# Where the last two projection steps stand among the token mixers' steps of a hybrid encoder

## Chip, cores and metric

The kernel runs on one core of a Trainium2 chip. The metric is the device time of one execution in microseconds (us), as a median over runs. Engines are called as in the profile: PE (TensorE matmuls), PEld (TensorE weight loads), DVE (VectorE), ACT (ScalarE), POOL (GpSimd), SP (SyncE, which issues most of the DMAs here).

## What is computed

Two layers, each over 512 tokens of width 1024. A layer projects its input x with one matrix `w_in`, gives the parts to three token mixers, joins their outputs with a second matrix, and ends in a mixture of experts. Cut to what matters here:

```python
for l in range(DEPTH):                                   # DEPTH = 2
    p = x @ w_in[l]
    c_q, c_kv, k_r, m_q, m_k, m_v, m_o, m_g, s_z, s_xbc, s_dt = split(p)
    y_a = mla(c_q, c_kv, k_r, ...)                       # attention, 8 heads
    y_b = mlstm(m_q, m_k, m_v, m_o, m_g, ...)            # ends: y = sigmoid(m_o) * layernorm(h)
    y_c = ssd(s_z, s_xbc, s_dt, ...)                     # ends: y = rmsnorm(y * silu(z)) over 2 groups
    x = layernorm(alpha * x + concat(y_a, y_b, y_c) @ w_out[l])
    x = layernorm(alpha * x + experts(x))
```

## The kernel before

Tokens are cut into NT = 4 tiles of 128. The transposed input x lies in the SBUF tensor `xt` (16 parts: 8 blocks of 128 features, each as a high part `xh[k]` and a rest `xl[k]`), and each fp32 product is built of three fp32r matmuls (high times high, high times rest, rest times high). All other large data live in 37 SBUF slots `s0` to `s36` (the profile calls them all `s`), handed out first in, first out; a slot taken from the pool and given back later in the program text is waited for by its next user. PSUM has 8 banks (`b` in the profile): banks 0 to 2 (`PA`) for projections and attention's inputs, banks 3 to 7 (`PB`) for the SSD, which the mLSTM (`PM`, banks 3 and 4) and attention's scores (`PT_`, banks 5 to 7) use after it.

The mixers are generator functions. One string, `SEQ`, written out by hand, says which generator goes one step further; it is the same for both layers:

```python
streams = {"d": ssd(), "p": projections(), "m": mlstm(), "i": mla_in(), "h": ssd_heads()}
for n, t in enumerate(SEQ):
    if t == "s" and "s" not in streams:
        streams["s"], streams["v"] = attention()
    next(streams[t], 1)
for t in "dphmisv":
    assert next(streams[t], 1) == 1
```

What the steps are (d17 is the 17th d of the string):

- d1 to d19, `ssd()`: d1 to d8 and d10 to d17 each take one token tile in one direction (ACT exponentials, a DVE product with the matrix C·B, two PE products into the bank `py`); d9 and d18 close a group (DVE: `y = x*d + py`, then `y * z2`; ACT: its square); d19 is the norm: `rms_cols` (one-column matmuls against `ones`), the DVE chain `rsqrt_`, `row_bc` (matmuls against `ident` that spread the result over partitions) and two DVE products. A d20 has nothing left to do.
- p1 to p11, `projections()`: p8 and p9 make mLSTM's v, two token tiles each, and p10 and p11 make `tho`, the tanh of mLSTM's output gate, two token tiles each: `proj_tm` is 24 matmuls of 256 columns per tile out of `xt` (written `b<-s,xt` in the profile), then an ACT tanh. At its begin p10 gives back the weights of v, fetches and splits the gate's weights. Its load from DRAM is issued at p8. A p12 only gives the four slots of the gate's weights back.
- i1 to i3, `mla_in()`: i1 holds the two `rms_cols` of attention's inputs, i2 loads and splits `w_ukv`, i3 makes the values `vt` (four times three matmuls of 512 columns, four ACT copies) and the router's sums. An i4 has nothing left to do.
- h1, `ssd_heads()`: splits the two SSD outputs into `xt` blocks 6 and 7, which p11 must have read to its end.
- m: mLSTM's 22 steps; m1 transposes the keys, the last one normalises and multiplies with `tho`. s and v: attention's scores and values, 40 steps each.

After the mixers the output projection `w_out` follows, then the router and the experts.

The order in which a single engine meets the instructions is laid out ahead of time by the framework's planner, for which the text's order is a rank among instructions that are ready by its own estimates; so the queue of an engine need not have the text's order.

Of the kernel before, what the change touches and what calls it, by code (L numbers as in the profile page):

```python
# [68 lines left out]
MA = 3  # L69
NM = 2  # L70
SSD_STEPS = 19
SEQ = 'dpddpdpdpddpdddpdpddpiddpidpiddpddphimmssmsmssmsvmsvvsmsvsmsmvssvsvvsvmmvsvsvsmvmsvsmsvmsvsvmvvsvmmsvsvsmssvvmsmsvsvmsvsvsvvssvsvvsvsvvvvvv'

ROPE_INV = [1.0, 0.5623413324356079, 0.3162277638912201, 0.17782793939113617, 0.10000000149011612,
            0.05623413249850273, 0.03162277489900589, 0.017782794311642647, 0.009999999776482582,
# [137 lines left out]
def tile_trunk(ctx: ExitStack, tc: tile.TileContext, ins, out, dbg=None, depth=DEPTH):  # L213
# [46 lines left out]
    def ph(n):  # L260
        if PHASE:
            PHASE(n)
            if n != lastp[0]:
                lows[lastp[0]] = [min(a, b.low) for a, b in zip(lows.get(lastp[0], [99] * 4), (pool, PA, PB))]
                pool.low, PA.low, PB.low = len(pool.whole), 9, 9
            if n == "comb":
                print(lows)
            lastp[0] = n
# [290 lines left out]
    for l in range(depth):  # L559
# [424 lines left out]
        def ssd_heads():  # L984
            for g in range(2):
                finish_heads(6 + g, yz[g].ap)
                yz[g].free()
            yield
# [404 lines left out]
        streams = {"d": ssd(), "p": projections(), "m": mlstm(), "i": mla_in(), "h": ssd_heads()}  # L1393
        for n, t in enumerate(SEQ):
            ph({"m": "mlstm", "d": "ssd", "p": "proj"}.get(t, "attn"))
# [834 lines left out]
```

## Time and profile before

| | |
|---|---|
| median of 3 runs | 1066.05 us (1061.36 to 1069.1) |
| profiled execution | 1070.26 us, span 1067.8 us, mean granted clock 0.974 |
| PE, PEld busy | 93%, 69% of the span |
| DVE, ACT, POOL busy | 78%, 60%, 25% of the span |
| DMA | mean 166 GB/s over the span |

A busy PE is not a PE at its peak, since matmuls overlap. The mixers' part that this document is about runs from some 110 to 288 us in the first layer, and from some 635 to 814 us in the second.

### The profile page before, as it was taken

To read this page: it belongs to the slowest core of one execution; us is meant where nothing else is said; L and a number is where in the kernel's file an instruction comes from. 1 tells how busy PE (TensorE), PEld (TensorE's weight loads), DVE (VectorE), ACT (ScalarE), POOL (GpSimd) and SP (SyncE) were. 2 spreads that over 40 slices of the span, in tenths; PEclk is the share of its full clock that TensorE was granted. 3 is DMA by queue.
4 is the path that set the end of the run, shared out by engine and by line. 5 is a ranking of instruction groups with operands and counts; after the bars stand their busy time and mean duration, and the time that the engine had idled before them with its cause. 6 is when DMAs were issued, how large, how long until landed. Compare 5 with 4: busy or idle time off the path is not lost. (4 is left out here: it accounts for less than half of the span.)

```text
span 1067.8 us, 15553 instructions
## 1 busy us (share of the span) xinstructions
PE 996.5 (93%) x5310; PEld 739.2 (69%) x5310; DVE 836.0 (78%) x1832; ACT 644.6 (60%) x1182; POOL 267.2 (25%) x232
## 2 busy tenths in 40 slices
PE   6999999988998999999999999999799989999995
PEld 6876788555687666666598768876466876666653
DVE  8995557787749799999969955577876498999996
ACT  5565646555524588888646564466464347778874
POOL 1000002223003255565100000022220123556652
PEclk9999989998999899999999998999999989999998
DMA  7211100132656889996532120011347477999933
GB/s 305 69 45 45 40 21 21 35 126 99 234 198 218 282 288 345 335 324 213 204 139 70 40 69 1 21 40 41 118 138 246 168 275 264 311 339 337 308 94 155
DMA packets 51795, 176.76 MB, mean 166 GB/s; under 512 B 8169, under 2 KB 8681, under 8 KB 51712
## 3 DMA queue, kind: packets, MB, share of 16 engines
q1 hardware_dynamic: 45216, 160.42, 42.2%
q0 software_dynamic: 6496, 15.31, 6.0%
q8 instruction: 42, 0.69, 0.3%
q14 instruction: 41, 0.34, 0.1%
HBM read 159.61 MB, written 23.59 MB: 172 GB/s over the span
## 5 line engine op out<-in xcount | busy, mean ns | idle before, releaser
L230 PE MATMUL b<-xt,s 128*128 128x512 f32 (+3 forms) x1484 | 327.1, 367 | 13.8 <-ACT s L230 8.6
L230 PE MATMUL b<-s,s 128*128 128x512 f32 (+7 forms) x1308 | 324.7, 404 | 14.0 <-ACT s L230 7.1
L230 PEld LDWEIGHTS b<-xt,s 128*128 128x128 f32 (+2 forms) x1484 | 234.0, 183 | 80.3 <-issue 11.5
L230 DVE TENSOR_TENSOR s<-s,s 128x1024 fp32r<-128x1024 f32 (+8 forms) x254 | 247.6, 1000 | 50.5 <-ACT s L230 41.7
L230 PEld LDWEIGHTS b<-s,s 128*128 128x128 f32 (+3 forms) x1308 | 185.0, 173 | 99.7 <-DVE s L230 22.6
L230 ACT ACTIVATE s<-b 128x512 f32<-128x512 f32 (+8 forms) x282 | 135.0, 496 | 191.2 <-PE b L230 182.3
L230 ACT ACTIVATE s<-s 128x1024 fp32r<-128x1024 f32 (+5 forms) x219 | 191.6, 910 | 85.1 <-DVE s L230 31.8
L230 PE MATMUL b<-s,xt 128*128 128x256 f32 (+2 forms) x944 | 209.1, 362 | 0.4 <-POOL s L1523 0.4
L230 PEld LDWEIGHTS b<-s,xt 128*128 128x128 f32 (+1 forms) x944 | 150.6, 192 | 34.7 <-issue 4.8
L230 DVE TENSOR_TENSOR xt<-s,xt 128x1024 fp32r<-128x1024 f32 (+1 forms) x106 | 118.3, 1122 | 13.8 <-ACT xt L230 13.7
L230 ACT ACTIVATE xt<-s 128x1024 fp32r<-128x1024 f32 (+1 forms) x107 | 110.4, 1042 | 26.1 <-PE b L230 17.7
L230 PE MATMUL b<-ident,s 128*128 128x128 f32 (+3 forms) x736 | 107.4, 273 | 18.6 <-POOL s L1338 7.7
L230 PEld LDWEIGHTS b<-ident,s 128*128 128x128 f32 (+3 forms) x736 | 81.5, 153 | 53.3 <-ACT s L230 13.9
L1598 POOL DMA_INDIRECT acc<-s,slx x28 | 55.3, 1976 | 99.3 <-ACT s L230 79.4
L230 ACT ACTIVATE s<-b,mx,qsc 128x512 f32<-128x512 f32 x64 | 49.7, 782 | 25.5 <-DVE mx L230 25.1
L1338 POOL TENSOR_SCALAR s<-s,sums 128x512 f32<-128x512 f32 x48 | 37.6, 788 | 105.7 <-DVE sums L230 93.6
L1094 POOL MEMSET s<- 128x780 f32 x4 | 3.0, 756 | 219.9 <-DVE s L230 186.3
L230 DVE TENSOR_REDUCE mx<-b 128x1 f32<-128x512 f32 x64 | 43.2, 686 | 18.3 <-PE b L230 17.9
L1446 POOL DMA_INDIRECT s<-x1d,slx x30 | 40.5, 1351 | 57.4 <-PE b L230 23.0
L230 DVE TENSOR_TENSOR s<-b,s 128x192 fp32r<-128x192 f32 (+3 forms) x92 | 46.9, 524 | 4.6 <-POOL s L1127 2.6
L230 PE MATMUL b<-xt 128*96 128x512 f32 x160 | 48.0, 406 | 1.4 <-DVE xt L230 1.4
L230 ACT ACTIVATE s<-b,slw 96x512 f32<-96x512 f32 (+1 forms) x60 | 39.1, 682 | 14.9 <-PE b L230 8.3
(254 smaller groups left out, 983.9 us busy)
## 6 DMA issues: line engine op xcount, KB each, us to landing
s<-in_w_gu_dram SPq DMA_DIRECT2D x128, 512.0 KB
s<-in_expert_w_down_dram SPq DMA_DIRECT2D x64, 512.0 KB
s<-in_w_inp_dram SPq DMA_DIRECT2D x36, 512.0 KB
s<-in_w_outp_dram SPq DMA_DIRECT2D x16, 512.0 KB
x1d<-s SPq DMA_DIRECT2D x8, 512.0 KB
acc<-s SPq DMA_DIRECT2D x8, 512.0 KB
s<-acc SPq DMA_DIRECT2D x8, 512.0 KB
s<-in_x_t_dram SPq DMA_DIRECT2D x4, 512.0 KB
```

The source lines that it names most:

```text
L230: r = f(*a, **kw)
L1094: G.memset(cb.ap, 0.0)
L1338: (V if hd in NORMV else G).tensor_scalar(P.ap, P.ap, sums, 0.0, op0=OP.mult, op1=OP.add)
L1446: self.ga = G.indirect_dma_start(out=self.xg[:BLK], out_offset=None, in_=x1d[0:128 * n, :], in_offset=bass.IndirectOffsetOnAxis(ap=ix[:BLK ...
L1598: G.indirect_dma_start(out=acc[:, :], out_offset=bass.IndirectOffsetOnAxis(ap=self.ix[:BLK, 0:1], axis=0), in_=yt[:BLK], in_offset=None, b ...
```

## The change

Only the string changes. Steps that stand in both texts before and behind the changed stretch are left out here:

```diff
-SEQ = 'dpddpdpdpddpdddpdpddpiddpidpiddpddphimmssmsm...'
+SEQ = 'dpddpdpdpddpdddpdpddpiddpiddddpiphmmssmsm...'
```

With the steps numbered, the stretch behind i2 is

```
before: ... p9 i2 d16 p10 i3 d17 d18 p11 d19 d20 p12 h1 i4 m1 m2 s1 s2 ...
after:  ... p9 i2 d16 d17 d18 d19 p10 i3 p11 h1 m1 m2 s1 s2 ...
```

p10, i3 and p11 keep their order among themselves. d17 and d18 go ahead of p10 and i3, and d19 goes ahead of all three. d20, p12 and i4 leave the string; the loop behind it runs them when all steps of attention and mLSTM are written. So the four slots of the gate's weights, given back ahead of h1 before, are given back at the end of the mixers.

## Rows read from the trace of the kernel before

**Rows 1.** The page's first part: busy time, share of the span, instructions.

```profile
PE 996.5 (93%) x5310; PEld 739.2 (69%) x5310; DVE 836.0 (78%) x1832; ACT 644.6 (60%) x1182; POOL 267.2 (25%) x232
```

**Rows 2.** Busy time by stretch: us, engines, granted clock, DMA share, GB/s.

```profile
132.00:144.00 12.00, 12.00 (x77) 11.77 (x76) 5.11 (x31) 3.02 (x9) 0.00 (x0) 0.72 0.00 1
144.00:163.00 19.00, 19.00 (x140) 16.37 (x139) 9.31 (x20) 9.60 (x26) 0.76 (x1) 1.00 0.08 29
...
163.00:186.00 23.00, 22.31 (x141) 18.09 (x139) 18.23 (x50) 15.82 (x43) 5.96 (x9) 1.00 0.07 24
186.00:232.00 46.00, 44.10 (x240) 29.55 (x241) 36.45 (x103) 25.12 (x64) 12.24 (x17) 1.00 0.25 81
232.00:251.00 19.00, 12.93 (x40) 6.99 (x37) 15.87 (x36) 9.50 (x16) 6.01 (x4) 0.73 0.22 78
...
688.00:711.00 23.00, 21.46 (x132) 17.44 (x130) 16.33 (x47) 14.27 (x39) 5.88 (x9) 1.00 0.07 24
...
760.00:777.00 17.00, 10.89 (x37) 5.66 (x34) 14.01 (x34) 8.90 (x16) 5.39 (x4) 0.80 0.18 62
```

**Rows 3.** Timeline of PE, first layer: start, length, line, operation, count.

```profile
132.44 3.08 PE L230 MATMUL b<-ones,s 128*128 128x1 f32 x24
135.38 1.84 PE L230 MATMUL b<-s,xt 128*128 128x256 f32 x7
137.02 0.63 PE L230 MATMUL b<-s,sel 128*128 128x512 f32 x1
137.45 4.34 PE L230 MATMUL b<-s,xt 128*128 128x256 f32 x20
...
148.68 4.73 PE L230 MATMUL b<-s,xt 128*128 128x256 f32 x38
153.25 2.92 PE L230 MATMUL b<-s,s 128*128 128x512 f32 x12
...
156.25 1.08 PE L230 MATMUL b<-s,s 128*64 128x512 f32 x4
157.26 6.00 PE L230 MATMUL b<-s,xt 128*128 128x256 f32 x48
163.09 1.84 PE L230 MATMUL b<-ones,s 128*128 128x1 f32 x16
...
165.18 2.57 PE L230 MATMUL b<-s,s 128*128 128x512 f32 x11
167.67 2.05 PE L230 MATMUL b<-ident,rq_y 128*128 128x128 f32 x16
```

**Rows 4.** Timelines of DVE and ACT there; idle time ahead in brackets.

```profile
157.38 0.75 DVE L230 SCALAR_TENSOR_TENSOR s<-s,par,b 128x512 f32<-128x512 f32 x1 [0.76 <-PE b L230]
158.16 0.69 DVE L230 TENSOR_TENSOR s<-s,s 128x512 f32<-128x512 f32 x1
...
158.94 0.63 ACT L230 ACTIVATE s<-s 128x512 f32<-128x512 f32 x1 [2.14 <-DVE s L230]
...
164.97 0.17 DVE L230 TENSOR_SCALAR rms<-b 128x8 f32<-128x8 f32 x1 [2.19 <-PE b L230]
...
167.46 0.15 DVE L230 SCALAR_TENSOR_TENSOR rq_y<-rq_t,rq_y 128x8 f32<-128x8 f32 x1
...
169.02 1.48 DVE L230 SCALAR_TENSOR_TENSOR s<-s,par,b 128x512 f32<-128x512 f32 x2
...
171.07 0.68 DVE L230 TENSOR_TENSOR s<-b,rot 128x512 f32<-128x512 f32 x1
```

**Rows 5.** Timeline of PE: waits early and late in attention, first layer.

```profile
176.89 1.86 PE L230 MATMUL b<-s,s 128*128 128x128 f32 x11 [0.61 <-ACT s L230]
...
240.20 0.47 PE L230 MATMUL b<-ident,s 128*128 128x128 f32 x2 [2.12 <-ACT s L230]
242.84 1.36 PE L230 MATMUL b<-ident,s 128*128 128x128 f32 x4 [2.17 <-POOL s L1338]
```

**Rows 6.** SP's timeline, first layer: the first load of `w_out`.

```profile
188.79 0.33 SPq L277 DMA_DIRECT2D s<-in_w_outp_dram  x1
```

More of the change, by code (lines that the diff above doesn't have):

```diff
@@ L71 @@
 SSD_STEPS = 19
-SEQ = 'dpddpdpdpddpdddpdpddpiddpidpiddpddphimmssmsmssmsvmsvvsmsvsmsmvssvsvvsvmmvsvsvsmvmsvsmsvmsvsvmvvsvmmsvsvsmssvvmsmsvsvmsvsvsvvssvsvvsvsvvvvvv'
+SEQ = 'dpddpdpdpddpdddpdpddpiddpiddddpiphmmssmsmssmsvmsvvsmsvsmsmvssvsvvsvmmvsvsvsmvmsvsmsvmsvsvmvvsvmmsvsvsmssvvmsmsvsvmsvsvsvvssvsvvsvsvvvvvv'
 ROPE_INV = [1.0, 0.5623413324356079, 0.3162277638912201, 0.17782793939113617, 0.10000000149011612,
```

## Prediction

> **What bounds the kernel now.** I read the page's busy shares first: PE is busy for 93% of the span, DVE for 78%, nothing else comes near [rows 1]. That is an average, so next came the busy time by stretch, cut where the mixers change their work [rows 2]. From 132 to 163 us of the first layer, where all the moved steps lie, PE is busy without a gap (12.00 of 12.00 and 19.00 of 19.00), while DVE works for 14.4 and ACT for 12.6 of the 31 us. From 163 to 186, where attention starts up, PE misses 0.69 us (22.31 of 23.00), and 1.54 us in the second layer (21.46 of 23.00). From 186 to 232 PE has 44.10 of 46.00. Then comes the one real hole, 232 to 251: PE 12.93 of 19.00 at a mean granted clock of 0.73, and the same in the second layer (10.89 of 17.00, clock 0.80). So the changed steps stand in a stretch that is full of PE work, and what follows them can only be late by what PE has to do or by a chain through other engines that PE can't cover.
>
> The second view is PE's timeline [rows 3], to see whether the queue follows the text. It doesn't. p8 to p11 are 48 matmuls each of the form `b<-s,xt` with 256 columns. Those of p9 are cut open by an SSD broadcast (`sel`, at 137.02) that belongs to a later step; i3's twelve matmuls (153.25) run before the four of d17 (156.25); d19's `row_bc` (167.67) runs behind the first eleven matmuls of attention (165.18). The text's order is a rank among what is ready, and PE is handed the projections wherever an SSD chain isn't ready yet.
>
> **What the change moves, and what each part costs.** Nothing is added or taken away: p10, i3 and p11 keep their order, and d17, d18 and d19 get a better rank.
>
> *p10 and p11*: 96 matmuls. 38 took 4.73 us, 124 ns each, so about 12 us of PE a layer, and p11's 48 took 6.00 us at one go [rows 3]. They read `xt` and weights split long before, so they are ready at any time. They have no DMA of their own to issue (the load is issued at p8) and nothing on POOL; on SP they pass no load. Cost of standing later: nothing, as long as something else fills PE, and the reverse is what has to be looked at.
>
> *d17 to d19*: PE 1.08 (d17's products), 1.84 (`rms_cols`), 2.05 (`row_bc`), together 4.97 us [rows 3]. DVE 0.75 + 0.69 for d18, 2.64 from the first to the last of the small operations of the square root (164.97 to 167.46 + 0.15), 1.48 for the two last products, together 5.56 us [rows 4]. They have no DMA and no POOL work. At present d17's products run at 156.25, d18 follows from 157.38 to 159.57 with ACT's square, and then `rms_cols` stands behind p11 until 163.09. After the change the chain runs under p10 and p11: `rms_cols` between about 155 and 158 (an estimate: the square ends where d17's products are no longer behind i3, some 3 us earlier), the root and `row_bc` behind it, all before p11 has ended.
>
> *The sum on PE up to attention's first matmul.* p11 now ends later by what went ahead of it, 1.84 + 2.05 us, at about 163.09 + 3.89 = 166.98. `rms_cols` was ahead of attention already (165.18), `row_bc` wasn't. So attention's first matmuls start about 2.05 us later than 165.18, and `row_bc`'s 2.05 us no longer stand at 167.67. PE's total up to there is the same: 0.
>
> *The sum on DVE there.* From 164.97 on DVE has d19's 2.64 and 1.48 us between attention's first steps, and the next step of head 0 (the product with `rot`) starts only at 171.07, 3.3 us after its eleven matmuls end at 167.75 [rows 3, 4]. After the change that work is done before; only h1's two splits remain, which wait for p11 in both texts. The eleven matmuls end at 169.8 (167.75 + 2.05), and the product can start between 170.2 and 170.9 behind the two splits. Head 0's chain is thus 0.2 to 0.9 us earlier than 171.07, not later. What this can buy at once is PE's missing time in the startup, 0.69 and 1.54 us [rows 2]; one such wait, 0.61 us for ACT, is seen at 176.89 [rows 5]. I take 0.5 us a layer, 1.0 us together, the middle between nothing and the 2.2 us of both stretches.
>
> *The four slots kept to the end.* Counted from the code, at least 9 of the 37 slots lie free at every point of attention before the change, so at least 5 after it. The slot that would be handed out with four fewer was given back at least 7 steps earlier from s1 on. I cost this at nothing; what hides it is the other free slots. Behind the mixers the slots for `w_out` and x come from younger places in the list. The first such load is issued at 188.79 [rows 6], and the matmuls it serves come after 250; even 30 us later it would be issued 30 us ahead of them. Were that cover gone, the cost would be one such load's wait; its lower bound is a gain of nothing, as DMA isn't what PE waits for in these stretches.
>
> *The sum.* 1070.26 us of the profiled execution (span 1067.8 and 2.5 around it) less 1.0 gives 1069.3. That execution was 4.2 us over the median of 1066.05, so against the median the forecast is **1065 us**, no change that a measurement can tell: I take 1% of the median, some 10.7 us, as what this kernel's runs (1061.36 to 1069.1) can tell from nothing.
>
> A rule speaks against the change. The Trainium skill, page "Perfetto Trace Analysis", section "Optimization Strategy", says that where the most contended engine changes between regimes, time may be won by interleaving them; the new text puts the SSD's last steps in a row and the projections alone behind them. By that rule the text loses some interleaving. The trace has the engines interleave whatever the text says [rows 3], so I give the rule only the chance of the first rival below.
>
> **Rivals.**
>
> *Slower: the SSD's last chain is uncovered.* If the queue puts d17 to d19 ahead without projections between them, PE waits for the chain: 1.08 + 0.75 + 0.69 + 0.63 + 1.84 + 2.64 + 2.05 = 9.68 us, of which PE works for 4.97 [rows 3, 4]; 4.7 us are open in each layer, 9.4 in both. It decides from the point at which less than 4.7 us of p10's and p11's 12 us stand inside the chain. On top, the clock may fall. It does so after i1's 24 one-column matmuls (3.08 us at 132.44), with a mean of 0.72 from 132 to 144 [rows 2, 3], that is part of the stretch at 1.2 GHz; there 20 projection matmuls took 4.34 us, 217 ns each against 124. A fall over 27 of them costs 2.5 us, 5 us in both layers. Together 14.4 us: 1080. For it: p10's tanh and i3's copies may now stand behind d18's square in ACT's queue, and the projections have only three banks to run ahead into. Against it: 12 us of work that is always ready, and a queue that cut p9 open for the same purpose. The fall alone, with d19's 16 one-column matmuls now among the projections, gives 1070; those 16 brought no fall where they were (clock 1.00 from 163 to 186).
>
> *Faster: the hole at 232 shrinks.* There PE waits 2.12 us for ACT and 2.17 us for POOL [rows 5], DVE is busy for 15.87 of 19 us and the clock goes down; mLSTM's last step and attention's late heads meet there. If head 0's lead moves their meeting, up to 6.07 + 6.11 us of missing PE time and the lost clock, 0.27 x 19 + 0.20 x 17 = 8.5 us, are at stake, 20.7 us; half of it with the startup's 2.2 gives 12.5 us: 1053 to 1054. Against it: between 186 and 232 PE is busy for 96%, and a lead of under 1 us is lost in that.
>
> *The change hardly does what it says.* The planner may lay out nearly the same queues, since d17's products weren't ready much before i3's. Then the time is 1066, which is the same class as my forecast.
>
> The page "Perfetto Trace Analysis", section "Identifying the Most-Contended Engine", says that the time PE spends on matmuls isn't a good measure, and that the busy share of weight loads is one. By it 144 to 163 is full enough (16.37 of 19, 86%), and 163 to 186 (18.09 of 23, 79%) has a little more room than the matmuls show, which would help the faster rival by more than the 0.69 us that I counted.
>
> **How the numbers follow.** Forecast with "hardly does what it says" 0.70 (1062 to 1070), the fall of the clock alone 0.06 (1070), uncovered chain 0.11 (1075 to 1081), smaller hole 0.13 (1050 to 1060). The range takes in the forecast, the fall and most of both outer cases: 1053 to 1078. Faster by over 1% (below 1055.4): 0.13, as a smaller hole of half size just reaches it and a planner's reshuffle may add; slower by over 1% (above 1076.7): 0.12; within: 0.75.
>
> **What would show it.** In the profile after: `ones` x16 and `ident,rq_y` x16 stand ahead of p11's end on PE, and between them projections (if not, the slower rival); PE still has 31 of 31 us there; DVE's square-root operations lie ahead of attention's first matmuls; the product with `rot` starts within 1 us of where it was; PE misses less than 0.69 and 1.54 us in the startup; the hole keeps some 6 us in each layer. The prediction is wrong if PE shows gaps before attention, if a second stretch at 1.2 GHz appears near d19, or if the hole is another size.

## The result and the profile after

The change makes the kernel slower: a median of 1073.74 us over nine runs (1067.44 to 1078.64) against 1064.08 us for the kernel before (nine runs, 1060.81 to 1069.1), a ratio of 1.0087 with a 95% interval of 1.0062 to 1.0111. By the ratio that is 9.3 us of 1064. I had forecast no change (1065). The time lies in the range that I gave, but the whole interval lies above 1: the kernel did get slower.

The profiled execution of after took 1067.44 us, the shortest of its nine runs, with a span of 1065.5 us and a clock of 0.977. Its span is thus shorter than the 1067.8 us of before, though the kernel is slower. The two spans can't be set against each other; the stages have to be compared one by one. First the stretches (columns as in [rows 2]) of after, first layer:

```profile
130.00:145.00 15.00, 14.90 (x125) 13.86 (x123) 8.85 (x40) 5.87 (x20) 0.00 (x0) 1.00 0.01 2
145.00:163.00 18.00, 18.00 (x131) 15.93 (x130) 8.11 (x24) 6.58 (x16) 1.51 (x2) 1.00 0.09 31
163.00:186.00 23.00, 22.01 (x127) 17.16 (x126) 18.84 (x47) 15.93 (x43) 6.96 (x9) 1.00 0.26 91
186.00:232.00 46.00, 44.22 (x234) 28.82 (x233) 37.90 (x101) 26.78 (x65) 12.37 (x16) 1.00 0.18 63
232.00:252.00 20.00, 12.81 (x41) 7.72 (x40) 12.43 (x36) 8.38 (x17) 4.08 (x4) 0.74 0.41 146
```

PE is full up to attention (14.90 of 15.00 and 18.00 of 18.00), as before. The first row holds a surprise: the clock is 1.00 here, where i1's one-column matmuls stood at a mean of 0.72 in before [rows 2]. The hole from 232 on is still there, and PE's 12.81 us of 20 are a little less than before's (13.93 of the same 20), while DVE does only 12.43 us in it instead of 15.87.

PE's timeline of after shows whether the queue does what the text says:

```profile
131.69 2.73 PE L230 MATMUL b<-ones,s 128*128 128x1 f32 x24
...
146.79 1.50 PE L230 MATMUL b<-s,s 128*64 128x512 f32 x4
148.22 2.53 PE L230 MATMUL b<-s,xt 128*128 128x256 f32 x19
150.58 0.99 PE L230 MATMUL b<-ones,s 128*128 128x1 f32 x8
151.43 1.43 PE L230 MATMUL b<-s,xt 128*128 128x256 f32 x10
152.70 2.23 PE L230 MATMUL b<-s,s 128*128 128x512 f32 x9
154.81 2.05 PE L230 MATMUL b<-ident,rq_y 128*128 128x128 f32 x16
...
157.53 5.95 PE L230 MATMUL b<-s,xt 128*128 128x256 f32 x48
164.11 5.06 PE L230 MATMUL b<-s,s 128*128 128x512 f32 x21
...
282.24 3.65 PE L230 MATMUL b<-s,s 128*64 128x512 f32 x14
285.82 14.99 PE L230 MATMUL b<-s,xt 128*128 128x512 f32 x63
...
301.96 1.07 PE L230 MATMUL b<-wrg,s 128*128 128x20 f32 x8
```

d17's products (146.79), half of d19's `rms_cols` (150.58; the other half stands at 141.92) and `row_bc` (154.81) stand between projections and ahead of p11 (157.53), and attention begins at 164.11. The lines from 282.24 on show where it is lost. The 14 matmuls `128*64` are attention's last values, and the router's first matmuls (`wrg`) stand at 301.96. Between them 63 matmuls of `w_out` run in one go (one more, at 301.52, already belongs to its second half). `w_out`'s first half has 96 matmuls, which by the code take the SSD's output first, then mLSTM's, then heads 0 to 3, then heads 4 to 7, 24 each. Most of the 63 therefore don't need attention's last heads, and could have filled PE's gaps *inside* attention's tail. In before the same place reads

```profile
284.41 3.65 PE L230 MATMUL b<-s,s 128*64 128x512 f32 x14
287.99 12.33 PE L230 MATMUL b<-s,xt 128*128 128x512 f32 x52
...
301.48 1.07 PE L230 MATMUL b<-wrg,s 128*128 128x20 f32 x8
```

52 are left over instead of 63. Eleven more at 0.238 us (14.99 / 63) are 2.6 us, and the tail from the end of the 14 matmuls to `wrg` grew from 13.4 to 16.1 us.

Why they were late is seen on the engines that split the fetched `w_out`: ACT makes the high part, and POOL (first and third block) or DVE (second and fourth) the rest. ACT, DVE, POOL and PE of before:

```profile
236.14 2.00 ACT L230 ACTIVATE s<-s 128x1024 f32<-128x1024 f32 x2
241.00 1.21 DVE L230 TENSOR_TENSOR s<-s,s 128x1024 fp32r<-128x1024 f32 x1
246.37 1.06 ACT L230 ACTIVATE s<-s 128x1024 fp32r<-128x1024 f32 x1 [1.27 <-issue]
247.57 2.38 POOL L410 TENSOR_TENSOR s<-s,s 128x1024 fp32r<-128x1024 f32 x1 [4.12 <-issue]
253.15 2.02 PE L230 MATMUL b<-s,xt 128*128 128x512 f32 x8
```

The same of after:

```profile
255.46 1.05 ACT L230 ACTIVATE s<-s 128x1024 fp32r<-128x1024 f32 x1
257.36 0.62 PE L230 MATMUL b<-s,xt 128*128 128x512 f32 x2
257.56 1.06 ACT L230 ACTIVATE s<-s 128x1024 fp32r<-128x1024 f32 x1 [0.15 <-PE b L230]
262.34 2.37 POOL L410 TENSOR_TENSOR s<-s,s 128x1024 fp32r<-128x1024 f32 x1 [3.66 <-PE b L230]
265.65 0.97 PE L230 MATMUL b<-s,xt 128*128 128x512 f32 x3
```

In before the first line holds two operations: mLSTM's square and, at 237.09, the first split. The second follows at 246.37. In after they come at 255.46 and 257.56, 18 and 11 us later. `w_out`'s first matmul is at 250.82 in before and at 257.36 in after. In after only two run before POOL has made the first block's rest (264.71), and the third is at 265.65; before has 11 of them done by 256.5.

What the first of them splits had been fetched long before; SP's timeline of after:

```profile
161.96 2.36 SPq L277 DMA_DIRECT2D s<-in_w_gu_dram  x4
...
209.96 11.33 SPq L277 DMA_DIRECT2D s<-in_w_outp_dram  x2
```

The first `w_out` loads go out at 209.96 instead of 188.79 [rows 6], still 45 us ahead of the split. So what is missing should be a free slot for the split's *output*; the experiments test that. And 161.96 shows who has the four slots that p12 used to return: the first expert's `w_gu`, whose first load goes out at 261.50 in before.

PE also lost clock behind the hole: from 252 to 292 the mean granted clock is 0.96 in after and 1.00 in before. How much of the loss that is, no run parts.

### The profile page after: what moved, and what is told of

Read it like the earlier page. It is cut to its first block, busy times and chain, and to the rows that moved or that the text cites. A ratio compares the mean times of both kernels' runs of the same rounds, so it can differ in the third digit from the quotient of the medians.

```text
span 1065.5 us, 15556 instructions
## 1 busy us (share of the span) xinstructions
PE 996.4 (94%) x5310; PEld 735.4 (69%) x5310; DVE 836.4 (79%) x1832; ACT 644.9 (61%) x1182; POOL 270.9 (25%) x232
## 5 line engine op out<-in xcount | busy, mean ns | idle before, releaser
L230 PE MATMUL b<-s,s 128*128 128x512 f32 (+8 forms) x1312 | 334.9, 410 | 14.6 <-DVE s L230 7.5
L230 ACT ACTIVATE s<-s 128x1024 fp32r<-128x1024 f32 (+6 forms) x219 | 191.4, 910 | 74.3 <-DVE s L230 31.9
L230 PE MATMUL b<-s,xt 128*128 128x256 f32 (+2 forms) x944 | 202.4, 354 | 0.5 <-POOL s L1523 0.4
L230 PEld LDWEIGHTS b<-s,xt 128*128 128x128 f32 (+1 forms) x944 | 145.5, 184 | 35.1 <-issue 5.6
```

Source lines behind the costliest of these rows:

```text
L230: r = f(*a, **kw)
```

## The experiments

Theory: the new order costs nothing; the loss comes from p12. Its four slots (the split weights of mLSTM's output gate) are out of the pool during all of attention. The pool hands out the oldest free slot first, so everything behind the mixers gets a slot that was given back later in the text, and the split parts of `w_out` (wo_split, eight slots for the first half) wait for later steps of attention and mLSTM. Rivals: the order itself (the uncovered chain, or d19 in another place); the loads of `w_out`, which are also later; and the early fetch of `w_gu`.

All were measured beside the kernel before on the same chip, so its median differs a little (1064.08 for after, 1065.34 for after again and e1 to e3, 1064.8 for e4 to e6). The ratios are the measured ones and not the quotients of these medians; for e1 the quotient would be 1.0018. Where a loss is given in us, it is what the ratio has over 1, times before's median, unless medians are named. To place a difference I read two stretches off PE's timeline in each layer: **A**, from i1's 24 one-column matmuls to the end of p11, and **B**, from there to the router's first `wrg` matmul, of which the **tail** is the part behind attention's last 14 value matmuls.

| | median, us | ratio to before | A, layers 1 / 2 | B | tail |
|---|---|---|---|---|---|
| before (profile) | | | 30.8 / 30.8 | 138.2 / 139.3 | 13.4 / 13.5 |
| after | 1073.74 | 1.0087 (1.0062 to 1.0111) | 31.8 / 31.8 | 138.5 / 138.7 | 16.1 / 16.1 |
| after, run again | 1076.21 | 1.0084 (1.0060 to 1.0108) | 34.5 / 33.0 | 137.6 / 138.7 | 16.1 / 16.1 |
| e1: slots back at once | 1067.26 | 1.0005 (0.9990 to 1.0021) | 31.8 / 32.9 | 135.2 / 135.7 | 11.8 / 11.8 |
| e2: old order, slots kept | 1071.08 | 1.0049 (1.0028 to 1.0069) | 28.1 / 29.3 | 140.9 / 142.4 | 14.4 / 14.4 |
| e3: slots to the front of the pool | 1068.06 | 1.0020 (1.0007 to 1.0034) | 31.8 / 32.9 | 136.5 / 135.5 | 11.8 / 11.8 |
| e4: slots to the split parts | 1069.23 | 1.0031 (1.0013 to 1.0049) | 31.8 / 31.8 | 134.7 / 134.8 | 11.8 / 11.9 |
| e5: slots to the loads only | 1073.82 | 1.0071 (1.0043 to 1.0099) | 34.5 / 33.0 | 137.9 / 139.0 | 15.4 / 15.4 |
| e6: e1, splits still earlier | 1076.05 | 1.0105 (1.0071 to 1.0138) | 31.8 / 31.8 | 139.5 / 139.1 | 13.5 / 13.5 |

A depends on the clock behind i1: with the clock at 1.00 it is 28.1 us in the old order and 31.8 in the new one; with the fall (0.77 from 130 to 145) it is 30.8 and 34.5. At the same clock the new order makes A 3.7 us longer. (The values between, 29.3 and 33, are second layers in which the clock was low for a shorter time.) B is what must give that back.

**e1, the order alone.** p12 is put right behind p11; d17 to d19 stay ahead of p10.

```diff
-...piddpiddddpiphmmss...
+...piddpiddddpipphmmss...   # the last p before h is p12
```

> The changed order of the steps, with the gate's four weight slots given back right behind p11, as before the change. Theory A (the kept slots are the cause): the loads and splits of w_out come back to the times they had before the change (the first w_out load near 190 us, the third and fourth near 225, not 236 and 245; the first w_out matmul near 251, not 257), and the time is that of the kernel before, ratio 0.997 to 1.003. Theory B (the order of d17 to d19 is the cause): the time stays with the changed kernel, ratio 1.006 to 1.011.

Measured: 1.0005, a tie with before. B is 3.0 and 3.6 us shorter than in before, A 3.7 longer at the same clock: together nearly nothing, as the sum on PE had it. The lines of e1 that answer to those above, PE's and then ACT's:

```profile
248.21 2.67 PE L230 MATMUL b<-s,s 128*128 128x512 f32 x5
250.81 3.07 PE L230 MATMUL b<-s,xt 128*128 128x512 f32 x12
...
283.63 3.65 PE L230 MATMUL b<-s,s 128*64 128x512 f32 x14
287.21 10.76 PE L230 MATMUL b<-s,xt 128*128 128x512 f32 x45
...
299.12 1.07 PE L230 MATMUL b<-wrg,s 128*128 128x20 f32 x8
```

```profile
228.38 1.06 ACT L230 ACTIVATE s<-s 128x1024 fp32r<-128x1024 f32 x1 [1.10 <-DMA s<-in_w_outp_dram]
233.96 1.99 ACT L230 ACTIVATE s<-s 128x1024 fp32r<-128x1024 f32 x2
```

The first split is at 228.38, `w_out` starts at 250.81, and 45 matmuls are left behind attention, 18 fewer than in after (18 x 0.238 = 4.3 us, the difference of the tails, 16.1 and 11.8). So the order of d17 to d19 and p10, p11 isn't what costs; the whole loss goes with p12. By the medians of the runs side by side, the place of p12 alone is worth 8.95 us (1076.21 for after again, 1067.26 for e1).

**e2, the kept slots alone.** The order of before, without d20, p12 and i4.

```diff
-...piddpidpiddpddphimmss...
+...piddpidpiddpdhmmss...
```

> The order of the steps as before the change, with the four slots kept to the end of the mixers. Theory A (kept slots): the whole loss shows here, ratio 1.006 to 1.011, with the third and fourth w_out load 10 to 20 us later than before. Theory B (order): ratio 0.997 to 1.003, whatever the loads do.

Measured: 1.0049, below the 1.006 to 1.011 that I had expected, but clear of 1. Keeping the slots costs in the old order too, 5.2 us against 9.3 in the new one. A of the first layer is at its old length (28.1 at full clock), and B is 2.7 and 3.1 us longer than in before, the tail 1.0 and 0.9 of that. Why the slots cost more in the new order than in the old one was not tested by itself; the count of steps under e3 has a hint.

**e3, the four slots to the front of the pool**, when the mixers are written: whoever comes next gets them first, rather than last.

```diff
 for t in "dphmisv":
     assert next(streams[t], 1) == 1
+pool.whole[:] = pool.whole[-4:] + pool.whole[:-4]
```

> The changed kernel with the four kept slots put at the front of the free list behind the mixers, so that the four loads of w_out's first half take them and are issued near 162 us. Theory A (kept slots push everything behind the mixers to younger slots): what follows stands four places older again, so the loss is gone, ratio 0.994 to 1.003. Theory B (order): ratio 1.006 to 1.011. A third theory, that the loads alone are late but the slots for the split parts don't matter, also gives 1.000 here; e1 and e3 do not tell it from A.

Measured: 1.0020; most of the loss is gone, with the four slots still kept through attention. Counted from the code, with m1 as step 1 and the last step of attention and mLSTM as step 102, the slots of the first four pairs of split parts had been given back at these steps:

| | first pair | second | third | fourth |
|---|---|---|---|---|
| before | 60, 60 | 60, 63 | 72, 74 | 85, 87 |
| after, e5 | 74, 85 | 87, 87 | 87, 88 | 88, 96 |
| e1, e3 | 60, 60 | 60, 63 | 74, 85 | 87, 87 |
| e2 | 72, 74 | 85, 87 | 87, 88 | 88, 96 |

In after the first pair is as late as the third and fourth were in before. e2's first pair is complete at step 74 and after's only at 85, and in their traces the first block's rest on POOL follows at 255.43 and 262.34: this may be why e2 loses less. Slots are not all, though. Before has the first two pairs as early as e1, yet leaves 52 matmuls over and not 45; why was not tested.

e3 gives earlier slots to the loads and to the split parts alike. The next two part them.

**e4, the four slots to the split parts only**; loads and x get the slots that they have in after.

```diff
+kept = pool.whole[-4:]                     # behind the loop over "dphmisv"
 ...
+pool.whole[:] = kept + [i for i in pool.whole if i not in kept]
 ps = [P4.get() for _ in range(NT)]
 for a, q in enumerate(order):
     w = wo_split(raws[0][a], a)
```

> The changed kernel, with the four kept slots put in front only where w_out's weights begin to be split, so that the first two splits write into them; w_out's four loads keep the young slots that they have in the changed kernel. Theory S (late slots for the split parts are what costs): the first w_out matmul comes back from 257 to near 251 us and the stretch from attention's last products to the router's first matmul from 16.1 to below 13.5 us; ratio 0.997 to 1.004. Theory L (late loads of w_out are what costs): the third and fourth load stay at 236 and 245 us and so does the loss; ratio 1.006 to 1.011.

**e5, the four slots to the loads only**; the split parts get the slots that they have in after.

```diff
+pool.whole[:] = pool.whole[-4:] + pool.whole[:-4]     # as e3
 ...
+young = [i for i in pool.whole if i not in pool.sound]
+pool.whole[:] = young[4:] + young[:4] + [i for i in pool.whole if i in pool.sound]
 for a, q in enumerate(order):
```

> The changed kernel, with the four kept slots for w_out's four loads (issued near 162 us), while the eight split parts of w_out's first half get just the slots that they have in the changed kernel. Theory S (split parts): the loss stays, the stretch from attention's end to the router stays near 16 us, ratio 1.006 to 1.011. Theory L (loads): the loss is gone, ratio 0.997 to 1.003.

Measured: e4 1.0031, e5 1.0071. e5, whose loads are the earliest of all, keeps most or all of after's loss; e4, whose loads are as late as after's, loses most of it. SP, ACT and PE of e5:

```profile
166.25 2.36 SPq L277 DMA_DIRECT2D s<-in_w_outp_dram  x4
```

```profile
259.07 1.04 ACT L230 ACTIVATE s<-s 128x1024 fp32r<-128x1024 f32 x1
```

```profile
286.66 3.65 PE L230 MATMUL b<-s,s 128*64 128x512 f32 x14
290.24 14.28 PE L230 MATMUL b<-s,xt 128*128 128x512 f32 x60
```

All four loads are out at 166.25, the split waits until 259.07 all the same, and 60 matmuls are left over. SP, ACT and PE of e4:

```profile
210.64 12.50 SPq L277 DMA_DIRECT2D s<-in_w_outp_dram  x2
238.27 7.39 SPq L277 DMA_DIRECT2D s<-in_w_outp_dram  x2
```

```profile
226.30 1.06 ACT L230 ACTIVATE s<-s 128x1024 fp32r<-128x1024 f32 x1
255.74 1.05 ACT L230 ACTIVATE s<-s 128x1024 fp32r<-128x1024 f32 x1
```

```profile
283.39 3.65 PE L230 MATMUL b<-s,s 128*64 128x512 f32 x14
286.97 10.73 PE L230 MATMUL b<-s,xt 128*128 128x512 f32 x45
```

Loads as late as in after, but the first split at 226.30, and 45 left over as in e1. So it is the slot for the split's output and not the load. e3 and e5 say it once more: by the count from the code both give the same slots to the loads, to x and to the norm's rows, and differ first in the split parts' slots, 1.0020 against 1.0071. Nor is it the early fetch of `w_gu`: in e5 it goes out from 259.84 on, and the loss stays. e4 is 3.3 us over before (4.4 by the medians) although its two stretches in the profile sum up to no loss; that rest is not explained.

**e6, splits earlier still**: e1, with the fetching of x and of the norm's parameters moved behind the first half's splits, so that these get the older slots.

```diff
 raws = [[wo_load(0, q) for q in order]]
-xr = load_x(ins["x"] if l == 0 else x2d)
-ln1 = load_ln(1)
 ...
+xr = load_x(ins["x"] if l == 0 else x2d)     # just ahead of the second half's loads
+ln1 = load_ln(1)
 raws.append([wo_load(1, q) for q in order])
```

> The changed order with the four slots given back at once (as in the first experiment), and the loads of x and of the norm's rows written behind the splits of w_out's first half, so that all eight split parts get slots given back at or before mLSTM's last step. Theory S: w_out's matmuls fill more of the hole at 232 to 260 us, the stretch from attention's end to the router falls below 11.8 us, and this is faster than both kernels, ratio 0.992 to 0.998. If banks or ACT and DVE, not slots, are the next bound there: ratio 0.998 to 1.002. If x then comes too late for the first sums: above 1.002.

Measured: 1.0105, slower, and no gain as I had hoped. Here three of the splits do come early, from 227.16 to 233.51 on ACT, but their second parts fall into the hole, where ACT, POOL and DVE carry the chain that PE waits for. POOL, DVE and PE of e6:

```profile
233.59 3.03 POOL L410 TENSOR_TENSOR s<-s,s 128x1024 fp32r<-128x1024 f32 x1 [3.53 <-ACT s L230]
237.86 2.35 POOL L410 TENSOR_TENSOR s<-s,s 128x1024 fp32r<-128x1024 f32 x1 [0.57 <-DVE va L230]
```

```profile
238.50 1.74 DVE L230 TENSOR_SCALAR rq_y<-va 128x16 int32<-128x16 int32 x1
```

```profile
252.20 3.54 PE L230 MATMUL b<-s,s 128*128 128x512 f32 x5 [1.42 <-ACT s L230]
255.67 3.25 PE L230 MATMUL b<-s,xt 128*128 128x512 f32 x9
```

`w_out` starts only at 255.67. Its first matmuls read the SSD's output, which was there long before; but in PE's queue they stand behind five of attention's matmuls, and these come at 252.20 instead of 248.21 in e1. From 252 to 292 the mean granted clock is 0.93 in e6, and 1.00 in e1. That the early splits disturb the hole is argued from these lines; no run parts the splits from the later loads of x.

**After, run once more**, unchanged, beside e1 and the others:

> The changed kernel once more on the same chip, to have its time and a second profile beside the others. Both theories: ratio 1.006 to 1.011. The hole at 232 to 260 us: PE misses some 8 us there, and the clock is low for some 13 us, in each layer; whether the clock falls behind i1's one-column matmuls is open, since it did in the kernel before and did not in the first profile of the changed one.

Measured: 1.0084, the same loss, and the clock's fall at i1 in the profile that the first one had not shown (0.77 from 130 to 145, against 1.00):

```profile
130.00:145.00 15.00, 15.00 (x102) 14.76 (x101) 7.53 (x36) 3.29 (x10) 0.00 (x0) 0.77 0.00 1
```

Twice 3.7 us for A, and the change of B in both layers (after +0.3 and -0.6), set against the measured differences, gives for after 7.1 against 9.3; e1 0.7 against 0.5; e2 5.8 against 5.2 (no change of A); e3 1.9 against 2.1; e5 6.8 against 7.6; e6 8.4 against 11.2; e4 -0.6 against 3.3. The two stretches hold most of every difference but e4's. In e4's profile the rest lies between the layers' stretches: from layer 1's first `wrg` matmul to layer 2's i1 it takes 362.5 us, before 356.7. But after's two profiles differ there by 5.0 us (354.7 and 359.6), so one profile of each can't settle it. None of the versions beats the kernel before; e1 ties with it.

## Why the prediction was wrong

*The order of PE's queue* was right: d17 to d19 run between projections, PE stays full from 145 to 163, and neither the uncovered chain nor a fall of the clock at d19's one-column matmuls happened (clock 1.00 from 145 to 163).

*The cost of p10 and p11 standing later, and the sum of 0 on PE up to attention* were right in size. p11 was to end 1.84 + 2.05 = 3.89 us later; at the same clock A is 3.7 us longer. Attention was to get the same back; in e1, where the slots return at once, B is 3.0 and 3.6 us shorter, and the run is a tie.

*The relief of DVE at attention's start* came only in part. The square root is done early, and attention's product with `rot` stands at 169.50 instead of 171.07 [rows 4]:

```profile
151.61 0.17 DVE L230 TENSOR_SCALAR rms<-b 128x8 f32<-128x8 f32 x1 [1.81 <-PE b L230]
...
169.50 0.69 DVE L230 TENSOR_TENSOR s<-b,rot 128x512 f32<-128x512 f32 x1
```

But in this profile the clock didn't fall at i1. In after's second profile, where it fell as in before, the product starts at 172.75, 1.7 us later than in before and not 0.2 to 0.9 earlier. Where d19 had left DVE room, mLSTM's small operations moved in: eight stand ahead of the product (2.47 us, from 170.25), where two did in before. I had left them out of that sum. PE has 22.01 of 23 us from 163 to 186, against 22.31, and 22.02 from 688 to 711, against 21.46 [rows 2]: 0.3 us gained over both layers, and not 1.0.

*The four slots kept to the end* is the step that failed: "I cost this at nothing; what hides it is the other free slots." I checked two things, that a slot is free at every point of attention, and that the first load of `w_out` still has time. Both hold, and both were beside the point. The pool has free slots, but it hands out the oldest first, and with four fewer in the round each request *behind* the mixers lands on a slot that was given back later. The first load went out 21 us later and still had 45 us of room; the split parts, which come behind x and the norm's rows in the same list, had none. The first two splits of `w_out` came 18 and 11 us later, 63 of its matmuls and not 45 were left behind attention's tail, and what was to go back from A to B didn't: B stayed at 138.5 and 138.7 us. "Were that cover gone, the cost would be one such load's wait" named the wrong user: e5 has the loads early, and 7.6 us of loss. Its price is 9.3 - 0.5 = 8.8 us with the new order, after against e1, and 5.2 us with the old one (e2). The term stood in the sum at 0.

*The hole at 232* I expected to keep its size, and nothing shows otherwise: from 232 to 252 PE has 12.81 us of 20 in after's first profile and 14.78 in its second, 13.93 in before and 14.58 in e1. `w_out` doesn't fill it: in none of the profiles does its first matmul of the first layer come before 250.24. What it fills are the gaps behind the hole.

*The range* (1053 to 1078) held the time by luck: it was that wide because of the rivals, and none of the three was what happened.

## What to carry to other kernels

Where buffers come from a first-in, first-out pool, a buffer that is returned later is paid for by everybody who asks afterwards: go through the later requests in order and compare, before and after, the step at which each one's buffer was given back, down to the small temporary parts and not only to the loads. The buffer that decides is the one whose user is filler for a later gap; such a loss showed here in no wait on a DMA, but in work left over behind the stretch that it should have filled, so count the matmuls there. And when a diff drops steps that "have nothing left to do" together with a change of order, run the two apart: here the order cost nothing that the runs can tell, and the dropped step was the whole cost.

## What was not expected of the hardware

Whether the clock falls behind i1's 24 one-column matmuls isn't fixed by the program. In before's profile it did in the first layer (0.77 from 130 to 145), in the two profiles of the very same kernel after once not (1.00) and once (0.77); A then takes 31.8 or 34.5 us, 2.7 us more for one layer. The stretch from 340 to 400, among the experts, had 0.97 in after's profile and 0.87 in e1's and e4's. Such differences add up to several us in a single profile, as much as the effect looked for here; so the medians of many runs decide about the time, and a profile only about the place.

Also, in e6 a DVE operation on 128x16 elements took 1.74 us (238.50) while POOL split a 128x1024 part (237.86 to 240.21); small operations of the square root otherwise take 0.16 to 0.17 us, as at 151.61 above. It isn't alone: beside POOL's splits in e1 (231.21 to 233.59 and 262.62 to 264.98) two DVE operations on 128x1024 elements took 2.81 us (231.87) and 2.74 us (263.32), where their like take 1.20 to 1.22. Each of the three ended only behind POOL's operation, 0.03, 1.08 and 1.08 us later, and e6's second layer has the same (764.37, 1.75 us). A maximum over a PSUM bank ran beside POOL's split at its usual 0.68 us (237.90). So some DVE operations seem to stand still while POOL splits, and others not; no run was made to test it.
